# One decoder layer on one Trainium2 core: the eight buffers for the weights' high and low parts each made 32 bytes longer

## The chip, the core and the metric

The kernel is one program on one core of a Trainium2 chip. The metric is the device time of one execution in microseconds (us). Before the change three runs gave 1734.22, 1735.92 and 1740.03 us; their median is 1735.92 us. The profile shown below comes from one further execution of 1733.97 us.

## The reference, cut to what is computed

One layer of a decoder on 256 tokens with 2048 channels, in float32. A vector `c` gives shifts, scales and gates (`ada`); a first sub-layer mixes tokens by softmax attention and by a gated delta rule; a second one is a SwiGLU of width 5632.

```python
mod = silu(c) @ w_ada + b_ada
sh1, sc1, g1, sh2, sc2, g2 = split(mod, 6)
h = x * (1 + sc1) + sh1
proj = h @ w_in                               # 2048 x 13344
y_a = moba_attention(q, k, v, rel_bias)       # 8 heads of 128
y_b = gated_delta_rule(...) * silu(z)         # 16 heads of 128
merged = sigmoid(gate_a) * (y_a @ w_proj_moba) + sigmoid(gate_b) * (y_b @ w_proj_gdn)
x = layer_norm(ALPHA * x + g1 * (merged @ w_out))
h = x * (1 + sc2) + sh2
gate, up = split(h @ w_ffn_in, 2)
x = layer_norm(ALPHA * x + g2 * ((silu(gate) * up) @ w_ffn_out))
```

## The kernel before

**Steps.** The large products run as a list of 572 steps (`prog`, run by `run(3)`). A step takes one block of a weight matrix, at most 128 partitions x 1024 numbers: `load_w` starts its transfer into a buffer `raw` (five of them), ScalarE rounds it to the high part `hi` (line 211, type fp32r), VectorE computes the rest `lo = raw - hi` (line 212), and TensorE multiplies with both. There are four buffers for `hi` and four for `lo`, used in turn, so step n uses `hi` and `lo` number n modulo 4. `run(3)` keeps the preparation about three steps ahead of the products. ScalarE can write the next `hi` only after TensorE has read the buffer's last contents.

**Products.** A matmul on TensorE has a *stationary* operand (128 columns, brought in by a weight load, shown as PEld) and a *moving* one (256 or 512 columns). Three helpers use the buffers:

- `ws_mm` (lines 291, 292, 293): the weights `hi` and `lo` are stationary, activations move, 256 columns. Three matmuls for each piece: `hi` by the activation's high part, `hi` by its low part, `lo` by its high part. The first sub-layer runs mostly here, with activations in tiles that the profile calls `s` (the high and low parts of the layer's input), `ya` (attention), `ybA`, `ybBh` and `ybBl` (delta rule).
- `ws_wide` (lines 298, 302): again stationary weights, with the SwiGLU's input `h` moving; 512 columns with `hi` (high and low part of `h` side by side), 256 with `lo`.
- `xs_unit` (lines 339, 340, 341): the activations (`s`, `mh`, `ml`, `ach`, `acl`) are stationary, the weights `hi` and `lo` move, 512 or 256 columns.

**Other work.** The order of each engine's work follows the order of the code, and smaller work (the convolutions, the delta rule, the attention, the `ada` sums of line 231) is fed in between steps by `tick`. SyncE issues the weights' transfers; GpSimd issues small ones.

**Places.** The buffers lie in a pool `wp` in the order five `raw`, four `hi`, four `lo`, after the pool `perm` and before the pools of the stages. A buffer of 1024 numbers has 4096 bytes per partition, so all thirteen begin at the same place modulo 4096. In the built program the places of the tiles that are multiplied are these, in bytes modulo 256 (those of the first line are what the change touches):

| tile | begins at, modulo 256 | role in the products |
|---|---|---|
| `hi` 0 to 3, `lo` 0 to 3 | 64, all eight | stationary on lines 291 to 302, moving on 339 to 341 |
| `raw` 0 to 4 | 64 | read by lines 211 and 212 |
| `s`, `h`, `ya` | 128 | moving (291 to 302); `s` also stationary (339 to 341) |
| `ybA`, `ybBh` | 64 | moving |
| `ybBl` | 96 | moving |
| `mh`, `ml`, `ach`, `acl` | 64 | stationary |

The pieces of a tile that one matmul reads begin at multiples of 512 or 1024 bytes from the tile's start, so each has its tile's place. (Only the blocks of 768 and of 512 numbers are shorter; their pieces keep the place too.)

Of the kernel before, what the change touches and what calls it, by code (L numbers as in the profile page):

```python
# [11 lines left out]
F32R = mybir.dt.float32r  # L12
# [6 lines left out]
P = 128  # L19
# [73 lines left out]
def layer(ctx, tc, a, out):  # L93
# [5 lines left out]
    wp = ctx.enter_context(tc.tile_pool(name="wp", bufs=3))  # L99
# [105 lines left out]
        return v  # L205

    def split_w(raw, kn, cn, pin=False):
        hi = wp.tile([P, 1024], F32R, tag="hi", name="hi", bufs=4)
        lo = wp.tile([P, 1024], F32R, tag="lo", name="lo", bufs=4)
        hi, lo = [t[:, :kn * cn].rearrange("p (k n) -> p k n", n=cn) for t in (hi, lo)]  # L210
        s_.copy(hi, raw)  # L211
        low = v_.tensor_tensor(lo, raw, hi.bitcast(F32), op=OP.subtract)  # L212
        if pin:
            tc.keep_in_program_order(low)
        return hi, lo
# [49 lines left out]
    def step(w, k0, kn, c0, cn, post, begun=0, pin=False):  # L265
        prog.append((lambda: split_w(load_w(w, k0, kn, c0, cn), kn, cn, pin), post, begun))
# [1049 lines left out]
```

## Time and profile before

| | |
|---|---|
| median of three runs | 1735.92 us |
| profiled execution, its time | 1733.97 us |
| profiled execution, its span | 1732.2 us |
| VectorE `lo` of 128x1024 (line 212), one | 1221 ns, 512 times |
| ScalarE `hi` of 128x1024 (line 211), one | 1050 ns, 512 times |
| `raw` of 512 KB, issue to landing | 4.3 to 5.4 us |
| bytes moved by DMA | 418.47 MB |

A page of the profile lists busy time by engine, then the span in 40 slices of 43.3 us, then the chain of work that ended last, then groups of instructions by line. The view of stretches gives, for a window of time, the busy time of an engine and in brackets how many of its instructions touch the window. Records of matmuls overlap, because a matmul is pipelined: one of 256 columns has a record of about 0.28 us, though the next begins some 0.12 us after it. What a matmul costs in a dense stretch is therefore the distance between starts, and it is read as the window's length divided by the number of matmuls that begin in it.

### The profile page before, as it was taken

The numbers are of one execution on the slowest core, as the hardware profiler recorded it, in microseconds if no ns is written. First come the engines' busy times: TensorE is split into PE (matmuls) and PEld (weight loads), VectorE is DVE, ScalarE is ACT, GpSimd is POOL, SyncE is SP. The second block draws the span as 40 slices with busy tenths as digits, with TensorE's granted clock in tenths as the row PEclk, the third lists the DMA queues.
The fourth block names the chain that finished last, engine by engine and source line by source line (L and its number), as shares of the span: only waits on it lengthen the run. The fifth ranks groups of instructions, "written<-read, shape, count | busy, mean of one in ns | idle before, by whom it ended". The sixth has DMA issues, their size and how long they took to land.

```text
span 1732.2 us, 28121 instructions
## 1 busy us (share of the span) xinstructions
PE 1666.6 (96%) x11109; PEld 1516.0 (88%) x11109; DVE 1234.5 (71%) x1763; ACT 816.5 (47%) x1125; POOL 39.5 (2%) x61
## 2 busy tenths in 40 slices
PE   3899999999999999999999999999999999999997
PEld 3898999889999778999978998888888888888896
DVE  6899987899656687467986787666666655455454
ACT  3544445868535435464434454444444444433341
POOL 0000010110100101000000000000000000000000
PEclk9999999999999999999999999999999999999998
DMA  9999996565767668677998468777777766765652
GB/s 362 335 365 344 348 330 222 180 205 168 240 219 237 201 211 296 205 231 259 317 349 276 157 204 269 238 240 240 239 238 236 234 189 192 236 195 191 195 183 84
DMA packets 114532, 418.47 MB, mean 242 GB/s; under 512 B 13388, under 2 KB 14396, under 8 KB 108892
## 3 DMA queue, kind: packets, MB, share of 16 engines
q1 hardware_dynamic: 109888, 401.16, 68.7%
q0 software_dynamic: 4512, 15.51, 3.4%
q8 instruction: 87, 1.43, 0.3%
q14 instruction: 45, 0.37, 0.1%
HBM read 409.18 MB, written 7.44 MB: 241 GB/s over the span
## 4 chain that ended last, share of the span: by engine, by line
PE 78%; DMA 7%; DVE 7%; issue 6%; ACT 1%; POOL 0%; DVEq 0%; ACTq 0%; SPq 0%; POOLq 0%
PE mm L298 17%; PE mm L291 9%; PE mm L293 9%; PE mm L302 8%; PE mm L292 8%; PE mm L340 7%; PE mm L341 7%; PE mm L339 7%; DVE lo L212 3%; DMA raw_a<-in_w_ada 2%; DMA r<-in_w_ada 1%; PE ps L692 1%; DMA raw<-in_w_out 1%; DVE r L231 1%; ACT hi L211 1%
## 5 line engine op out<-in xcount | busy, mean ns | idle before, releaser
L211 ACT CAST hi<-raw 128x1024 fp32r<-128x1024 f32 (+2 forms) x572 | 581.6, 1020 | 777.5 <-PE mm L341 201.6
L212 DVE TENSOR_TENSOR lo<-raw,hi 128x1024 fp32r<-128x1024 f32 (+2 forms) x572 | 672.3, 1183 | 274.3 <-ACT hi L211 271.2
L291 PE MATMUL mm<-s,hi 128*128 128x256 f32 x1184 | 338.3, 286 | 6.3 <-ACT hi L211 6.1
L293 PE MATMUL mm<-s,lo 128*128 128x256 f32 x1184 | 332.9, 282 | 6.6 <-DVE lo L212 6.4
L292 PE MATMUL mm<-s,hi 128*128 128x256 f32 x1184 | 332.4, 281 | 0.0
L298 PE MATMUL mm<-h,hi 128*128 128x512 f32 x1280 | 319.0, 391 | 0.0
L298 PEld LDWEIGHTS mm<-h,hi 128*128 128x128 f32 x1280 | 228.8, 188 | 39.4
L291 PEld LDWEIGHTS mm<-s,hi 128*128 128x128 f32 x1184 | 224.7, 190 | 11.6 <-ACT hi L211 8.5
L293 PEld LDWEIGHTS mm<-s,lo 128*128 128x128 f32 x1184 | 223.7, 189 | 9.6 <-DVE lo L212 8.6
L292 PEld LDWEIGHTS mm<-s,hi 128*128 128x128 f32 x1184 | 224.7, 190 | 0.2
L302 PEld LDWEIGHTS mm<-h,lo 128*128 128x128 f32 x1280 | 171.1, 188 | 13.2
L302 PE MATMUL mm<-h,lo 128*128 128x256 f32 x1280 | 174.1, 278 | 0.0
L340 PE MATMUL mm<-lo,ach 128*128 128x512 f32 (+1 forms) x440 | 152.6, 347 | 0.2 <-DVE lo L212 0.2
L339 PE MATMUL mm<-hi,ach 128*128 128x512 f32 (+1 forms) x440 | 152.6, 347 | 0.0
L341 PE MATMUL mm<-hi,acl 128*128 128x512 f32 (+1 forms) x440 | 152.6, 347 | 0.0
L231 DVE CUSTOM_DVE_ANT_0 raw_a<-raw_a,cb,cols 128x1024 f32<-128x1024 f32 x56 | 71.8, 1282 | 73.9 <-DMA raw_a<-in_w_ada 73.9
L231 DVE CUSTOM_DVE_ANT_0 raw_a<-raw_a,cb,ada_half 128x1024 f32<-128x1024 f32 x56 | 71.8, 1282 | 66.0 <-DMA raw_a<-in_w_ada 65.8
L231 DVE CUSTOM_DVE_ANT_0 r<-r,cb,cols 128x2048 f32<-128x2048 f32 x40 | 93.8, 2346 | 13.4 <-DMA r<-in_w_ada 13.3
L340 PEld LDWEIGHTS mm<-lo,ach 128*128 128x128 f32 x440 | 83.3, 189 | 11.1 <-DVE lo L212 0.7
L339 PEld LDWEIGHTS mm<-hi,ach 128*128 128x128 f32 x440 | 83.3, 189 | 10.4
L341 PEld LDWEIGHTS mm<-hi,acl 128*128 128x128 f32 x440 | 83.3, 189 | 10.1
L340 PE MATMUL mm<-lo,s 128*128 128x512 f32 x192 | 77.4, 403 | 3.9 <-DVE lo L212 3.9
(299 smaller groups left out, 2310.6 us busy)
## 6 DMA issues: line engine op xcount, KB each, us to landing
raw<-in_w_ffn_in SPq DMA_DIRECT2D x176, 512.0 KB, 4.3
raw<-in_w_in SPq DMA_DIRECT2D x168, 512.0 KB, 4.6
raw_a<-in_w_ada SPq DMA_DIRECT2D x112, 512.0 KB, 4.5
raw<-in_w_ffn_out SPq DMA_DIRECT2D x88, 512.0 KB, 4.3
r<-in_w_ada SPq DMA_DIRECT2D x40, 1024.0 KB, 8.2
raw<-in_w_proj_gdn SPq DMA_DIRECT2D x32, 512.0 KB, 4.6
raw<-in_w_out SPq DMA_DIRECT2D x32, 512.0 KB, 5.4
raw<-in_w_in SPq DMA_DIRECT2D x40, 384.0 KB, 5.5
```

What stands on the lines that cost most here:

```text
L211: s_.copy(hi, raw)
L212: low = v_.tensor_tensor(lo, raw, hi.bitcast(F32), op=OP.subtract)
L231: v_.tensor_tensor_reduce(out=raw, in0=raw, in1=cb[:, n * part:n * part + n], scale=1.0, scalar=cols[:, col:col + 1] if first else h, op0= ...
L291: t_.matmul(o, hi[:, i, c], ah, start=(first and i == 0 and t == 0), stop=False)
L292: t_.matmul(o, hi[:, i, c], al, start=False, stop=False)
L293: t_.matmul(o, lo[:, i, c], ah, start=False, stop=(last and i == kn - 1 and t == 1))
L298: t_.matmul(box[t].rearrange("p (u i) -> p u i", u=2), hi[:, i, t * P:(t + 1) * P], both[k0 + i], start=(first and i == 0), stop=False)
L302: t_.matmul(box[t][:, :S], lo[:, i, t * P:(t + 1) * P], both[k0 + i][:, 0, :], start=False, stop=(last and i == kn - 1))
L339: t_.matmul(box[h], xh, hi[:, i, :], start=start, stop=False)
L340: t_.matmul(box[h], xh, lo[:, i, :], start=False, stop=False)
L341: t_.matmul(box[h], xl, hi[:, i, :], start=False, stop=stop)
L692: t_.matmul(ps[:, n, :], lhs(n), rhs(n), start=True, stop=True)
```

## The change

Each of the eight buffers for `hi` and `lo` gets 1032 numbers instead of 1024, that is 32 bytes more per partition. The steps use the first `kn * cn` numbers as before.

```diff
     def split_w(raw, kn, cn, pin=False):
-        hi = wp.tile([P, 1024], F32R, tag="hi", name="hi", bufs=4)
-        lo = wp.tile([P, 1024], F32R, tag="lo", name="lo", bufs=4)
+        hi = wp.tile([P, 1032], F32R, tag="hi", name="hi", bufs=4)
+        lo = wp.tile([P, 1032], F32R, tag="lo", name="lo", bufs=4)
         hi, lo = [t[:, :kn * cn].rearrange("p (k n) -> p k n", n=cn) for t in (hi, lo)]
         s_.copy(hi, raw)
         low = v_.tensor_tensor(lo, raw, hi.bitcast(F32), op=OP.subtract)
```

The places in the built program after it, modulo 256:

| tile | before | after |
|---|---|---|
| `hi` 0, 1, 2, 3 | 64, 64, 64, 64 | 64, 96, 128, 160 |
| `lo` 0, 1, 2, 3 | 64, 64, 64, 64 | 192, 224, 0, 32 |
| all other tiles | | the same place (those behind the pool lie 256 bytes further) |

On every engine and on both queues for transfers the instructions, their order, their sizes and the semaphores they wait for are the same as before; they differ in addresses alone.

## The prediction

> **What bounds the kernel now.** I read the page first, from the top, then the stretches of TensorE.
>
> ```profile
> PE 1666.6 (96%) x11109; PEld 1516.0 (88%) x11109; DVE 1234.5 (71%) x1763; ACT 816.5 (47%) x1125; POOL 39.5 (2%) x61
> ```
>
> Then its part on the chain of work that ended last:
>
> ```profile
> PE 78%; DMA 7%; DVE 7%; issue 6%; ACT 1%; POOL 0%; DVEq 0%; ACTq 0%; SPq 0%; POOLq 0%
> ```
>
> Then the view of stretches, TensorE alone (window, length, busy and count of matmuls, clock, DMA share, GB/s):
>
> ```profile
> 0.00:160.00 160.00, 124.35 (x958) 0.99 0.93 347
> 160.00:1010.00 850.00, 831.52 (x6084) 0.99 0.74 246
> 1010.00:1460.00 450.00, 449.61 (x2664) 1.00 0.73 233
> 1460.00:1710.00 250.00, 249.75 (x1346) 1.00 0.58 189
> ```
>
> TensorE is busy in 96% of the span, has 78% of the chain that ended last, and is granted a clock of 0.99 and 1.00 in the stretches below. These say where: in the first 160 us it is busy for 124, with the DMA engines at 0.93, so transfers set the pace there; in the next 1550 us it has 831.5 + 449.6 + 249.8 = 1531 of them. A change of a nanosecond in each matmul after 160 us is therefore a change in the time; one in VectorE or ScalarE is mostly covered.
>
> The change moves no instruction, so the only question is whether an instruction's duration depends on the *places* of its operands. The next rows answer that for today's places: dense stretches of one kind each.
>
> ```profile
> 208.00:280.00 72.00, 72.00 (x614) 1.00 0.85 298
> 187.00:200.00 13.00, 13.00 (x117) 1.00 0.94 348
> 282.00:292.00 10.00, 10.00 (x91) 1.00 0.59 177
> 618.00:660.00 42.00, 42.00 (x182) 1.00 0.75 240
> 836.00:841.00 5.00, 5.00 (x44) 1.00 0.96 312
> 914.00:952.00 38.00, 38.00 (x169) 1.00 0.82 273
> 953.00:975.00 22.00, 22.00 (x185) 1.00 0.59 192
> ...
> 1496.00:1652.00 156.00, 156.00 (x690) 1.00 0.62 200
> 1655.00:1665.00 10.00, 10.00 (x86) 1.00 0.51 172
> ```
>
> In order: `s` moving over stationary `hi`/`lo` (256 columns), the same again a little earlier and a little later, `hi`/`lo` moving over stationary `s` (512), `ybA` moving over `hi`/`lo` (256), `hi`/`lo` over `mh` (512, then 256), and over `ach` (512, then 256). Some 2.4 records of 0.28 us (1.7 of the 0.39 us ones) begin ahead of a window and count in it; I take them off. The distance between starts is then 72/611.6 = **117.7 ns**, 13/114.6 = **113.4**, 10/88.6 = **112.9**, 42/180.3 = **232.9**, 5/41.7 = **119.9**, 38/167.3 = **227.1**, 22/182.6 = **120.5**, 156/688.3 = **226.6**, 10/83.6 = **119.6**. The clock is 1.00 in all of them. So the same form of matmul runs at more than one pace. What goes with it is how the two operands lie to each other. Take the place modulo 128 and call 0 to 63 the lower half, 64 to 127 the upper one. Today `hi` and `lo` are all upper; `ybA`, `mh`, `ach` are upper as well, and with them the pace is constant, 120 and 226.7. `s`, `h` and `ya` are lower, and with them it is 117.7 or 113.4, and 232.9. The SwiGLU's steps show the last pairing, `h` (lower) moving over `hi` and `lo` (upper):
>
> ```profile
> 1201.53 1.07 PE L302 MATMUL mm<-h,lo 128*128 128x256 f32 x8
> 1202.44 1.99 PE L298 MATMUL mm<-h,hi 128*128 128x512 f32 x8
> 1204.27 1.11 PE L302 MATMUL mm<-h,lo 128*128 128x256 f32 x8
> ```
>
> Eight matmuls in a row of start and length; without the last record's own length the seven distances are (1.07 - 0.28)/7 = 113 ns, then (1.11 - 0.28)/7 = 119 (mean 116) in the next step, and (1.99 - 0.39)/7 = 229 for 512 columns. The pace alternates by step with equal operands modulo 256, so it also depends on how a stretch is entered. The halves are my reading of these rows, not a proof.
>
> **The change part by part.** VectorE and ScalarE first: they read `raw` and write `hi` and `lo` at new places.
>
> ```profile
> L211 ACT CAST hi<-raw 128x1024 fp32r<-128x1024 f32 (+2 forms) x572 | 581.6, 1020 | 777.5 <-PE mm L341 201.6 <-PE mm L298 199.2 <-PE mm L292 197.5
> ...
> L1027 DVE SCALAR_TENSOR_TENSOR r<-xs,rt 128x512 f32<-128x512 f32 (+1 forms) x10 | 5.8, 576 | 0.1
> ...
> L1027 DVE SCALAR_TENSOR_TENSOR r<-r,rt 128x512 f32<-128x512 f32 (+1 forms) x10 | 5.5, 578 | 0.1
> ```
>
> On line 1027, in the two stages that use it, one input of VectorE begins at 96 (`xs`) or at 128 (`r`): 576 and 578 ns. Places cost VectorE nothing within 2 ns; over 572 `lo` that is 1.1 us of either sign, and it lies under TensorE. ScalarE, of which no pair of rows differs in place alone, sits idle for 777.5 us ahead of line 211, mostly because TensorE still reads the buffer; over 572 `hi` it would have to lose more than 1.3 us in each to fill that. I take 0 for both. `raw` stays where it was, so its transfers cost 0 as well; in the first 160 us these hide whatever the 934 matmuls there gain or lose.
>
> For TensorE I carry the halves over. After the change `hi` 0, 1 and `lo` 0, 1 are upper (64, 96), `hi` 2, 3 and `lo` 2, 3 lower (0, 32), so half of the steps change their pairing. Counts are from these rows and their like (`ya`, `ybA`, `ybBh`, `ybBl` have 128 in each row, `h` on lines 291 to 293 112, `mm_kept` 96, `ach`/`acl` at 256 columns 176, `mh`/`ml` 96 and 64); the last row counts the matmuls with `s` of the first 160 us:
>
> ```profile
> L291 PE MATMUL mm<-s,hi 128*128 128x256 f32 x1184 | 338.3, 286 | 6.3 <-ACT hi L211 6.1
> L293 PE MATMUL mm<-s,lo 128*128 128x256 f32 x1184 | 332.9, 282 | 6.6 <-DVE lo L212 6.4
> L292 PE MATMUL mm<-s,hi 128*128 128x256 f32 x1184 | 332.4, 281 | 0.0
> L298 PE MATMUL mm<-h,hi 128*128 128x512 f32 x1280 | 319.0, 391 | 0.0
> L302 PE MATMUL mm<-h,lo 128*128 128x256 f32 x1280 | 174.1, 278 | 0.0
> ...
> L341 PE MATMUL mm<-hi,acl 128*128 128x512 f32 x264 | 102.7, 389 | 0.0
> L339 PE MATMUL mm<-hi,s 128*128 128x512 f32 x192 | 78.6, 411 | 0.3 <-ACT hi L211 0.3
> ...
> 0.00:160.00 160.00, 119.83 (x934) 0.99 0.93 347
> ```
>
> 1. `s`, `h`, `ya` over `hi`/`lo`, 256 columns: 3 x 1184 and 1008 like them are 4560, less the 934 of the first 160 us = 3626. Half go from unequal to equal halves: 1813 x (119.9 - 117.7 = 2.2 ns) = **+4.0 us**.
> 2. `h` over `lo`: 640 x (119.9 - 116 = 3.9 ns) = **+2.5 us**.
> 3. `h` over `hi`, 512: 640 x (226.7 - 229) = **-1.5 us**.
> 4. `ybA`, `ybB` (768): 384 from equal to unequal, x (-2.2) = **-0.8 us**.
> 5. `hi`/`lo` over `s` (576): 288 x (226.7 - 232.9) = **-1.8 us**.
> 6. `hi`/`lo` over `ach`, `acl`, `mh`, `ml`, 512 (1080): 540 from equal to lower moving over upper stationary, which is the pairing of `h` over `hi`, 229: 540 x 2.3 = **+1.2 us**.
> 7. The same with 256 columns (720): 360 x (-2.2) = **-0.8 us**.
>
> The sum is 4.0 + 2.5 - 1.5 - 0.8 - 1.8 + 1.2 - 0.8 = **+2.8 us**, so 1733.97 becomes 1736.8 in the terms of the profiled execution. That execution is 1.95 us below the median of the runs; against the median the forecast is 1735.92 + 2.8 = **1738.7 us**, no change that a measurement of this kernel can tell (about 0.3%, 5.2 us).
>
> Not in that sum is a start that is 32 bytes off a multiple of 64, which half of the buffers get. The nearest rows are a moving and a stationary operand at 96:
>
> ```profile
> 879.74 0.28 PE L292 MATMUL mm<-ybBl,hi 128*128 128x256 f32 x1
> ...
> 880.70 0.28 PE L291 MATMUL mm<-ybBh,hi 128*128 128x256 f32 x1
> ```
>
> ```profile
> L692 PEld LDWEIGHTS ps<-TT,ma 128*128 128x128 f32 (+1 forms) x128 | 11.8, 165 | 7.6 <-DVE kqn L583 4.2 <-ACT sgb L965 2.6 <-DMA TT<-ubd 0.4
> ...
> L692 PEld LDWEIGHTS ps<-UU,z 128*128 128x128 f32 (+1 forms) x128 | 11.5, 163 | 0.5
> ```
>
> With every third moving operand at 96 (`ybBl`), eight matmuls take 0.96 us, 120 ns each as with `ybA`; and a weight load of `z`, at 96, takes 163 ns against 165 for `ma` at 64. I take 0. But the first row has a pace with room in it (120, where 113.4 is possible) and the second is another type, so the price is open: up to one step between the paces seen, 119.9 - 113.4 = 6.5 ns, on one side, and on the other a gain of the same size where a stretch falls into the faster pace.
>
> A rule that speaks against any effect: the Trainium skill, page "SBUF — State Buffer", section "Who interferes with whom", gives TensorE two independent read ports, one for the moving operand and one for weight loads, and says that it never waits on anyone. By that rule the places are worth nothing and the time stays 1735.9; the rows above, 113.4 to 120 ns for one form at one clock, do not look like it.
>
> **The rivals.**
>
> *Places mean nothing.* The paces would come from the lengths and order of the stretches alone, and all terms are 0: 1735.9 us. For it: `s` over `hi` runs at both 117.7 and 113.4 with equal places. Against it: 120 and 226.7 appear only where the halves are equal.
>
> *Faster: the fast pace spreads.* Today a stretch at 117.7 keeps that pace for as long as it is dense (611 matmuls in the row at 208), because every step repeats the same places; with new places at each step the pace is chosen anew each time, as in the SwiGLU, where every other step has 113. If half of term 1's matmuls fall to 113.4: 1813 x -4.3 = -7.8, in place of +4.0, with the other terms at -1.2: 1735.9 - 9.0 = 1727 us. If all do: -15.6 - 1.2, 1719 us. It beats the 0.3% from about 900 of the 3626.
>
> *Slower: a start 32 bytes off costs.* Half of the 9330 matmuls that the seven terms count read a `hi` or `lo` at 32, 96, 160 or 224. At 3.25 ns, half of 6.5: 4665 x 3.25 = +15 us, with the sum of 2.8 it gives 1754 us; at the full 6.5 ns +30, 1769. With the +2.8 it passes 0.3% from (5.2 - 2.8)/4665 = 0.5 ns. Against it: the rows of `ybBl` and `z`. For it: they are the only ones, and neither is tight.
>
> *The change doesn't do what it says.* The places in the built program are the intended ones, and no other tile changes place; I give this nothing.
>
> **How the numbers follow.** Forecast 0.36; nothing at all 0.08; faster 0.26; slower 0.30. The first two are within 0.3%: 0.44 together. The predicted time is the forecast's, 1738.7. The range takes in the faster rival to 1720 and the slower one to 1758, a price of some 4 ns; beyond them I leave about 0.07 and 0.10. The forecast's own range is 1734 to 1741.
>
> **What would show it.** In the profile after, the count of matmuls in a dense stretch of `s` over `hi`/`lo` gives the pace by step: right if steps alternate in pairs between 118 and 120; the faster rival if many are at 113; the slower if steps with `hi` 1 and 3 differ from those with 0 and 2. `ach` at 512 should alternate between 227 and 229, `hi` over `s` between 233 and 227. Lines 211 and 212 should keep their mean (1020 ns for line 211) within 3 ns. Wrong would be a pace outside 113 to 120 and 226 to 236, or a longer line 212 that TensorE waits for.

## The result, and the profile after

| | before | after |
|---|---|---|
| median of the runs | 1735.21 us (1734.22 to 1740.03, 5 runs) | 1749.84 us (1748.46 to 1756.02, 5 runs) |
| profiled execution, its time | 1733.97 us | 1756.02 us |
| ratio, with its 95% interval | | 1.0073 (1.0051 to 1.0095) |

The changed kernel is slower by 14.6 us, 0.7%. The forecast was 1738.7 us, no change; the time lies in the range, on the side of the rival that had 0.30. The profiled execution is the slowest of the five, so its own 22 us over before hold some 7 that the median doesn't show.

The page after: first the span, the busy times and the chain of work that ended last.

```profile
span 1754.2 us, 28121 instructions
...
PE 1684.4 (96%) x11109; PEld 1524.8 (87%) x11109; DVE 1235.2 (70%) x1763; ACT 815.2 (46%) x1125; POOL 39.6 (2%) x61
...
PE 74%; DVE 9%; issue 8%; DMA 7%; ACT 1%; POOL 0%; SPq 0%; DVEq 0%; ACTq 0%; POOLq 0%
...
L211 ACT CAST hi<-raw 128x1024 fp32r<-128x1024 f32 (+2 forms) x572 | 580.9, 1019 | 800.4 <-PE mm L341 212.8
L212 DVE TENSOR_TENSOR lo<-raw,hi 128x1024 fp32r<-128x1024 f32 (+2 forms) x572 | 673.1, 1184 | 304.2 <-ACT hi L211 300.8
...
L298 PE MATMUL mm<-h,hi 128*128 128x512 f32 x1280 | 323.2, 394 | 0.0
...
L302 PE MATMUL mm<-h,lo 128*128 128x256 f32 x1280 | 176.8, 280 | 0.0
```

Same instructions, and TensorE alone has grown: 17.8 us more busy, while VectorE and ScalarE stay within 1.3. Lines 211 and 212 take 1019 and 1184 ns; they took 1020 and 1183. Lines 298 and 302, with no wait ahead of them before or after, take 394 and 280 ns in place of 391 and 278. A matmul's own duration overlaps the next, so its price is read from how many start in a stretch. Here are three stretches without idle time at a clock of 1.00, of before (window, length, busy and count, clock, DMA share, GB/s): `s` moving over `hi`/`lo` with 256 columns; the SwiGLU's, half 512 columns (`h` over `hi`) and half 256 (`h` over `lo`); `hi`/`lo` moving over `ach`/`acl` with 512.

```profile
213.00:279.00 66.00, 66.00 (x562) 1.00 0.84 295
1055.00:1470.00 415.00, 415.00 (x2412) 1.00 0.72 230
1500.00:1650.00 150.00, 150.00 (x664) 1.00 0.61 196
```

And of the changed kernel:

```profile
213.00:279.00 66.00, 66.00 (x557) 1.00 0.82 293
1055.00:1470.00 415.00, 415.00 (x2374) 1.00 0.72 229
1500.00:1650.00 150.00, 150.00 (x648) 1.00 0.59 197
```

With the records that began ahead of a window taken off as in the prediction (2.4, 2 and 1.7), one matmul takes 66/559.6 = 117.9 ns before and 66/554.6 = 119.0 after; 415/2410 = 172.2 and 415/2372 = 175.0; 150/662.3 = 226.5 and 150/646.3 = 232.1. The SwiGLU alone loses 2.8 ns x 2560 = 7 us, about half of the 14.6. Below, these three windows serve as the measure of every kernel, and "the three paces" are worked out from them in this way.

### The profile page after: what moved, and what is told of

It is laid out like the page before. It is cut to its first block, busy times and chain, and to the rows that moved or that the text cites. A ratio compares the mean times of both kernels' runs of the same rounds, so it can differ in the third digit from the quotient of the medians.

```text
span 1754.2 us, 28121 instructions
## 1 busy us (share of the span) xinstructions
PE 1684.4 (96%) x11109; PEld 1524.8 (87%) x11109; DVE 1235.2 (70%) x1763; ACT 815.2 (46%) x1125; POOL 39.6 (2%) x61
## 4 chain that ended last, share of the span: by engine, by line
PE 74%; DVE 9%; issue 8%; DMA 7%; ACT 1%; POOL 0%; SPq 0%; DVEq 0%; ACTq 0%; POOLq 0%
PE mm L298 17%; PE mm L302 9%; PE mm L291 8%; PE mm L293 8%; PE mm L292 7%; PE mm L340 7%; PE mm L341 7%; PE mm L339 7%; DVE lo L212 3%; DMA raw_a<-in_w_ada 2%; PE ps L692 1%; DVE r L231 1%; DMA raw<-in_w_out 1%; DMA raw<-in_w_proj_gdn 1%; DMA r<-in_w_ada 1%
## 5 line engine op out<-in xcount | busy, mean ns | idle before, releaser
L211 ACT CAST hi<-raw 128x1024 fp32r<-128x1024 f32 (+2 forms) x572 | 580.9, 1019 | 800.4 <-PE mm L341 212.8
L212 DVE TENSOR_TENSOR lo<-raw,hi 128x1024 fp32r<-128x1024 f32 (+2 forms) x572 | 673.1, 1184 | 304.2 <-ACT hi L211 300.8
L298 PE MATMUL mm<-h,hi 128*128 128x512 f32 x1280 | 323.2, 394 | 0.0
L293 PEld LDWEIGHTS mm<-s,lo 128*128 128x128 f32 x1184 | 224.2, 190 | 11.1 <-DVE lo L212 10.1
L302 PEld LDWEIGHTS mm<-h,lo 128*128 128x128 f32 x1280 | 173.6, 188 | 13.7
L231 DVE CUSTOM_DVE_ANT_0 r<-r,cb,cols 128x2048 f32<-128x2048 f32 x40 | 93.7, 2347 | 12.3 <-DMA r<-in_w_ada 12.3
L340 PEld LDWEIGHTS mm<-lo,ach 128*128 128x128 f32 x440 | 82.8, 188 | 11.7
L341 PEld LDWEIGHTS mm<-hi,acl 128*128 128x128 f32 x440 | 82.7, 188 | 11.7
```

What stands on the lines that cost most here:

```text
L231: v_.tensor_tensor_reduce(out=raw, in0=raw, in1=cb[:, n * part:n * part + n], scale=1.0, scalar=cols[:, col:col + 1] if first else h, op0= ...
L293: t_.matmul(o, lo[:, i, c], ah, start=False, stop=(last and i == kn - 1 and t == 1))
L298: t_.matmul(box[t].rearrange("p (u i) -> p u i", u=2), hi[:, i, t * P:(t + 1) * P], both[k0 + i], start=(first and i == 0), stop=False)
L302: t_.matmul(box[t][:, :S], lo[:, i, t * P:(t + 1) * P], both[k0 + i][:, 0, :], start=False, stop=(last and i == kn - 1))
L340: t_.matmul(box[h], xh, lo[:, i, :], start=False, stop=False)
L341: t_.matmul(box[h], xl, hi[:, i, :], start=False, stop=stop)
```

## The experiments

Three theories were on record. 'Halves' is the forecast's: what counts is in which half of 128 bytes the two operands begin. 'Offset' is the slower rival's: a start that is no multiple of 64 costs. 'Variety' (later 'changing places'): the places as such cost nothing, but going to another one does. The edits below are against the kernel before; `gap(tag, n)` allocates once a tile of n elements of 4 bytes that nothing reads or writes, so what lies behind it moves.

### Only the later tiles move (gap256)

```
     lo = wp.tile([P, 1024], F32R, tag="lo", name="lo", bufs=4)
+    gap("gap2", 64)
```

> An unused tile of 256 bytes lies behind the eight buffers, which themselves keep their places (all at 64 modulo 256); every other tile lies exactly where the change puts it. It asks whether the 256 bytes by which the later pools moved have a part in the loss. Theory 'offset' (a start that is not a multiple of 64 bytes costs), theory 'variety' (it costs when the place changes from one operand to the next) and theory 'halves' (equal or unequal halves of 128 bytes) all expect 0 against before (within 0.2%). If it shows the change's +0.7%, all three fall.

Measured: 1736.85 us against 1736.88, ratio 0.9999 (0.9984 to 1.0015). The SwiGLU's window:

```profile
1055.00:1470.00 415.00, 415.00 (x2412) 1.00 0.72 228
```

The same count as before. The 256 bytes by which the change pushes other tiles have no part in the loss.

### All eight at 96, all eight at 128 (all96, all128)

```
+    gap("gap0", 8)
     hi = wp.tile([P, 1024], F32R, tag="hi", name="hi", bufs=4)
     lo = wp.tile([P, 1024], F32R, tag="lo", name="lo", bufs=4)
+    gap("gap2", 56)
```

That is all96; all128 has 16 and 48.

> All eight buffers at one place, 96 modulo 256; all other tiles as in the changed kernel. Offset: the change has half of its buffers off a multiple of 64 and lost 14.6 us, so with all of them off it loses about 29 us (+1.7%). Variety: all operands of a kind have one place again, 0 (within 0.3%), with a constant pace in each stretch. Halves: 96 lies in the upper half as 64 does, 0.

> All eight buffers at one place, 128 modulo 256; all other tiles as in the changed kernel. Offset: 0. Variety: 0. Halves: all eight change from the upper to the lower half, twice the seven terms of the prediction, 2 x 2.8 = +5.6 us (+0.3%), with a pace of 120 ns for 256 columns of s over hi, 226.7 ns for hi over s at 512 columns and 229 ns for hi over ach.

Measured: at 96 1744.31 us, ratio 1.0039 (1.0024 to 1.0055), +7.4 us; at 128 1746.96, ratio 1.0063 (1.0043 to 1.0083), +10.1 us. The windows at 96:

```profile
213.00:279.00 66.00, 66.00 (x569) 1.00 0.82 292
1055.00:1470.00 415.00, 415.00 (x2373) 1.00 0.71 226
1500.00:1650.00 150.00, 150.00 (x645) 1.00 0.59 196
```

And at 128:

```profile
213.00:279.00 66.00, 66.00 (x552) 1.00 0.83 292
1055.00:1470.00 415.00, 415.00 (x2381) 1.00 0.71 228
1500.00:1650.00 150.00, 150.00 (x657) 1.00 0.60 194
```

The three paces are 116.5, 175.0, 233.2 at 96, and 120.1, 174.4, 228.9 at 128. No theory stands whole. Nothing changes between steps, yet both are slower, so 'variety' is not all. 'Halves' is right that 96 and 128 differ, and for `s` (equal halves at 128: 120) and `ach` (unequal: 229), but not in its 0 for 96. 'Offset' is right for `ach` at 512 columns, where 96 costs the full step of 6.7 ns over 226.5, and wrong for `s` at 256, where 96 is faster than 64 (116.5 against 117.9); hence +7 and not +29.

### `hi` in steps of 64, `lo` at 64 (hi64steps)

```
-    hi = wp.tile([P, 1024], F32R, tag="hi", name="hi", bufs=4)
+    hi = wp.tile([P, 1040], F32R, tag="hi", name="hi", bufs=4)
```

> hi alone in four places that are all multiples of 64 bytes (64, 128, 192, 0 modulo 256); lo at 64 in all four buffers; all other tiles as in the changed kernel. Offset: 0, no start is off a multiple of 64. Variety: two of three matmuls read hi, so the larger part of the change's loss, +7 to +14 us (+0.4 to 0.8%). Halves: the terms of hi alone, about 0.

Measured: 1741.1 us, ratio 1.0024 (1.0007 to 1.0041), +4.2 us. Two of its windows, `s` and `ach`:

```profile
213.00:279.00 66.00, 66.00 (x572) 1.00 0.84 296
...
1500.00:1650.00 150.00, 150.00 (x649) 1.00 0.60 195
```

`s` at 66/569.6 = 115.9 ns is faster than before, `ach` at 231.7 slower, though no start is off a multiple of 64. It lies between the theories; it doesn't tell whether the places or their change do it.

### All at 160; and two places in turn (all160, alt192, alt128, alt96)

all160 is all96 with 24 and 40 elements. The other three give even steps one place and odd steps another (`count` begins as `[0]`):

```
+    par = count[0] % 2
+    count[0] += 1
+    if par:
+        gap("gap1", 32)
-    hi = wp.tile([P, 1024], F32R, tag="hi", name="hi", bufs=4)
-    lo = wp.tile([P, 1024], F32R, tag="lo", name="lo", bufs=4)
+    hi = wp.tile([P, 1024], F32R, tag=f"hi{par}", name="hi", bufs=2)
+    lo = wp.tile([P, 1024], F32R, tag=f"lo{par}", name="lo", bufs=2)
+    if par:
+        gap("gap2", 32)
```

That is alt192 (64 and 192); alt128 has 16 and 48, alt96 8 and 56.

> All eight buffers begin at 160 (32 modulo 128): 32 bytes off a multiple of 64, as 96 is, but in the lower half of 128, as 128 is. Theory 'own place, offset': what counts is whether the start is a multiple of 64; 160 then behaves as 96 did: 116.7 ns a matmul at 256 columns and 233.3 at 512 throughout, +7 us over before. Theory 'own place, half': the half of 128 counts, and 160 behaves as 128 did: 119 to 120 ns for s, h and ya, 118 for ach, 228 to 230 at 512, +10 us. Theory 'changing places' says nothing of this kernel, in which no step differs from the next.

> Both parts of even steps at 64, of odd steps at 192: the place changes by 128 bytes with each step. Theory 'own place modulo 128': the two are the same place, 0 us, paces as before (117.4 for s, 226.8 for ach at 512, 233.3 over s). Theory 'own place modulo 256': 192 is a place not seen yet, and something other than 0. Theory 'changing places' in its wide form (any change of buffer place between two steps breaks up the pace that a stretch keeps): +8 us, what the changed kernel lost (+14) beyond the mean of its places (about +6). In its narrow form (only a change modulo 128 counts): 0.

> Both parts of even steps at 64, of odd steps at 128. Theory 'own place': half of the steps cost what all of them cost with all eight at 128 (+10 us), so +5 us, and the paces are the mean of the two: 118.6 for s at 256 columns, 227.9 for ach at 512. Theory 'changing places': that and some 8 us more, +13 us, with ach at 512 at 230 or above, though neither place alone gives more than 229.

> Both parts of even steps at 64, of odd steps at 96. Theory 'own place': half of what all eight at 96 cost (+7 us), so +3.7 us; s at 117.1, ach at 512 at 230, the mean of 226.8 and 233.3. Theory 'changing places': some 8 us more, +12 us; s at 118 or above, though neither place alone gives more than 117.4.

Measured, with the ratio: all160 1750.17 us, 1.0087 (1.0062 to 1.0111), +13.6; alt192 1739.4, 1.0022 (1.0004 to 1.0039), +2.8; alt128 1740.81, 1.0021 (1.0008 to 1.0035), +4.2; alt96 1744.72, 1.0054 (1.0036 to 1.0071), +8.1. The windows at 160:

```profile
213.00:279.00 66.00, 66.00 (x560) 1.00 0.83 294
1055.00:1470.00 415.00, 415.00 (x2361) 1.00 0.72 227
1500.00:1650.00 150.00, 150.00 (x644) 1.00 0.61 194
```

The paces are 118.4, 175.9, 233.5: at 512 columns those of 96, as 'offset' had it, at 256 between those of 96 and 128; in time it is the slowest place measured. The SwiGLU and `ach` with 64 and 192 in turn:

```profile
1055.00:1470.00 415.00, 415.00 (x2383) 1.00 0.71 227
1500.00:1650.00 150.00, 150.00 (x653) 1.00 0.60 194
```

with 64 and 128 in turn:

```profile
1055.00:1470.00 415.00, 415.00 (x2398) 1.00 0.72 228
1500.00:1650.00 150.00, 150.00 (x652) 1.00 0.61 194
```

and with 64 and 96:

```profile
1055.00:1470.00 415.00, 415.00 (x2389) 1.00 0.72 227
1500.00:1650.00 150.00, 150.00 (x650) 1.00 0.61 197
```

For 64 and 128 the mean of the two places alone would be 173.3 and 227.7; measured are 415/2396 = 173.2 and 150/650.3 = 230.7. For 64 and 96: 173.6 and 229.8; measured 173.9 and 231.4. In time the means are +5.0 and +3.7, measured +4.2 and +8.1. So 'own place' holds for the SwiGLU; at 512 columns over `ach` the alternation adds 1.6 to 3 ns. In time 64 and 128 come out as 'own place' says. 64 and 96 lie between the theories: the interval, 6.2 to 12.3 us, leaves out the 3.7 of 'own place' and takes in the 12 of 'changing places'. Nor does `s` keep to the mean. Its window with 64 and 192 in turn, then with 64 and 128:

```profile
213.00:279.00 66.00, 66.00 (x581) 1.00 0.85 297
```

```profile
213.00:279.00 66.00, 66.00 (x568) 1.00 0.85 296
```

That is 114.1 ns, as with all eight at 192 (below), and 116.7, faster than 64 alone and 128 alone (117.9 and 120.1).

alt192 is not 0 in its paces (174.3 and 230.3): either 192 is not the place that 64 is, or the change by 128 bytes does it. The next kernel separates these.

### All at 192; a place for each stage (all192, bystage)

all192 is all96 with 32 and 32 elements. bystage gives each step an offset into longer buffers that all begin at 64 (in elements: 32 is place 192, 16 is 128, 8 is 96):

```
-    def split_w(raw, kn, cn, pin=False):
-        hi = wp.tile([P, 1024], F32R, tag="hi", name="hi", bufs=4)
-        lo = wp.tile([P, 1024], F32R, tag="lo", name="lo", bufs=4)
-        hi, lo = [t[:, :kn * cn].rearrange("p (k n) -> p k n", n=cn) for t in (hi, lo)]
+    def split_w(raw, kn, cn, pin=False, at=(32, 32)):
+        hi = wp.tile([P, 1088], F32R, tag="hi", name="hi", bufs=4)
+        lo = wp.tile([P, 1088], F32R, tag="lo", name="lo", bufs=4)
+        hi, lo = [t[:, o:o + kn * cn].rearrange("p (k n) -> p k n", n=cn) for t, o in zip((hi, lo), at)]
...
+            n = 8 if cn == 256 else 16 if ops is h_ops else 0
-            step(w, k0, kn, c0, cn, post)
+            step(w, k0, kn, c0, cn, post, at=(n, n))
...
-            step(w_fi, k, 4, c0, 256, post)
+            step(w_fi, k, 4, c0, 256, post, at=(0, 32))
...
-    nc = bacc.Bacc("TRN2", target_bir_lowering=False, num_devices=1, dynamic_dma_scratch_size=4096)
+    nc = bacc.Bacc("TRN2", target_bir_lowering=False, num_devices=1, dynamic_dma_scratch_size=2304)
```

> All eight buffers begin at 192, which is 64 modulo 128, so that no step differs from the next. Theory 'own place modulo 128': the same place as before, 0 us, paces as before (s at 256 columns 117.4 ns, ach at 512 226.8, h at 512 228.9). Theory 'own place modulo 256': the paces that the steps at 192 had where places alternated, now throughout: s 114.6, ach at 512 232.6, h at 512 233.0, s at 512 229.5; 3637 x -2.8 for s, 1637 x -0.6 for h, 366 x -2.7 for ya and 762 x -1.7 for yb are -13.5 us, 791 x 5.8, 270 x 4.3, 1280 x 4.1 and 526 x -3.8 are +9.0, together about -5 us. Theory 'changing places': what 64 and 192 in turn cost came from the change, so 0 us here.

> A place for each stage, the same for all its steps: 192 where hi and lo are the stationary part at 256 columns (s, ya, yb, h over lo), 96 where they move at 256 columns, 128 where they move over s at 512, 64 for the other 512-column matmuls, as before. The buffers are 256 bytes longer for it, and the descriptor ring of the DMA queue of POOL smaller. Theory 'own place': the paces add up by place: 3637 x -2.8 ns for s, 366 x -2.7 for ya, 762 x -1.7 for yb, 1637 x -0.6 for h are -13.5 us, less 934 x 2.8 = 2.6 that the transfers of the first 160 us hide; 718 x -3.3 at 96 -2.4, 526 x -5.6 at 128 -2.9: -16 us, about 1720. Theory 'own place modulo 128': 192 is 64, so only the last two terms, -5 us. Theory 'changing places': the place changes only where a stage ends, so as 'own place' says.

Measured: all192 1739.87 us, ratio 1.0021 (0.9996 to 1.0045), +4.3; bystage 1733.59, ratio 0.9976 (0.9954 to 0.9998), -2.0. The windows at 192:

```profile
213.00:279.00 66.00, 66.00 (x581) 1.00 0.85 297
1055.00:1470.00 415.00, 415.00 (x2395) 1.00 0.72 229
1500.00:1650.00 150.00, 150.00 (x647) 1.00 0.59 194
```

The paces are 114.1, 173.4, 232.5, without any change between steps: 192 is not 64, though the two are equal modulo 128. That ends 'halves'. The time does not follow these paces: 'own place modulo 256' expected about -5 us, and the distances, summed over all groups of matmuls, are about 6 us shorter than before, but the time is +4.3 us (interval -0.7 to +7.8).

Nor does a place alone fix the pace of `s`. A later stretch of all192, again `s` over `hi`/`lo` and nothing else:

```profile
704.00:727.00 23.00, 23.00 (x198) 1.00 0.63 211
```

This is 23/195.6 = 117.6 ns, the pace that `s` mostly has at 64; and the prediction has a row at 64 with 113.4. In the records of both kernels a long dense stretch of `s` has the one pace or the other from its start to its end. At 192 the faster comes more often: the mean over all records of `s` is 115.0 ns there and 117.4 at 64. At 96, 128 and 160 (116.9, 119.9, 118.3) no such pair of paces shows.

The windows of bystage:

```profile
213.00:279.00 66.00, 66.00 (x581) 1.00 0.86 297
1055.00:1470.00 415.00, 415.00 (x2420) 1.00 0.73 232
1500.00:1650.00 150.00, 150.00 (x663) 1.00 0.61 197
```

`s` at 192 has 114.1 here as well, and `ach` at 64 has 226.8, as before, though these buffers lie at other addresses and 256 bytes further apart: the place modulo 256 can be chosen for each stage, and the mean pace comes with it (over all records `s` has 115.3 here). Summed over all groups of matmuls, the distances between starts are 18 us shorter than before (counted as in the table of terms further down). But of the 16 us expected the runs show 2. The stage from 442 to 788 us, where the GDN heads are worked off between the projections, in bystage:

```profile
442.00:788.00 346.00, 326.29 (x2408) 0.98 0.70 227
```

and before:

```profile
442.00:788.00 346.00, 334.32 (x2440) 0.99 0.72 230
```

TensorE is busy for 8 us less there and still gets through 32 matmuls fewer. The waits of TensorE (waiter, what it waited for: us in total, times, longest) name the largest new one, in bystage:

```profile
PE ps L693 <- DMA TT<-ubd: 12.5, 2, 9.6
```

The same line before:

```profile
PE ps L692 <- DMA TT<-ubd: 0.2, 1, 0.2
```

That is 12.3 us more. The granted clock falls in the stretch of the longest of these waits, of bystage:

```profile
670.00:683.00 13.00, 3.88 (x19) 0.61 0.96 336
```

The mean granted clock of its timed runs was lower too, 0.987 against 0.991 for the kernel before beside it; its fastest run, 1720.34 us, is the one with 0.993.

Faster matmuls reach the transfer earlier, but it is not shown that this is the whole reason for the wait: this kernel also has the smaller descriptor ring of POOL's queue, on which the transfer is issued. Two issues of GpSimd (start, length, the issue, idle time before it), in bystage:

```profile
667.91 0.90 POOL L684 DMA_DIRECT2D UU<-ubd  x1 [6.96 <-issue]
668.80 0.90 POOL L684 DMA_DIRECT2D TT<-ubd  x1
```

And before:

```profile
665.20 0.91 POOL L683 DMA_DIRECT2D UU<-ubd  x1
670.06 0.89 POOL L683 DMA_DIRECT2D TT<-ubd  x1 [3.95 <-DMA ubd<-mt]
```

In bystage both transfers come after 6.96 us of idle time for which the profile shows no cause, one right behind the other. All three kernels with the smaller ring (the next two have it too) show such idle time there, 6.0 to 7.0 us, and the longest waits for `TT`, 9.8 to 12.5 us; no kernel with the old ring shows it, and their waits are at most 7.0 us (6.9 in all192). So the ring is a rival for a part of the lost gain. A run with the longer buffers and the old ring was not made.

### The changed kernel's places, changing each step or every eighth (each1, each8)

```
...
+    at = 8 * (count[0] % 4)
+    count[0] += 1
-    hi = wp.tile([P, 1024], F32R, tag="hi", name="hi", bufs=4)
-    lo = wp.tile([P, 1024], F32R, tag="lo", name="lo", bufs=4)
-    hi, lo = [t[:, :kn * cn].rearrange("p (k n) -> p k n", n=cn) for t in (hi, lo)]
+    hi = wp.tile([P, 1088], F32R, tag="hi", name="hi", bufs=4)
+    lo = wp.tile([P, 1088], F32R, tag="lo", name="lo", bufs=4)
+    hi, lo = [t[:, o:o + kn * cn].rearrange("p (k n) -> p k n", n=cn) for t, o in ((hi, at), (lo, at + 32))]
...
-    nc = bacc.Bacc("TRN2", target_bir_lowering=False, num_devices=1, dynamic_dma_scratch_size=4096)
+    nc = bacc.Bacc("TRN2", target_bir_lowering=False, num_devices=1, dynamic_dma_scratch_size=2304)
```

That is each1; each8 has `8 * (count[0] // 8 % 4)`.

> The places of the changed kernel in another way: the eight buffers begin at 64, and step n reads and writes hi at 64 + 32 x (n mod 4) and lo 128 bytes further on, which are the changed kernel's places step by step. (Buffers 256 bytes longer, the descriptor ring of POOL's DMA queue smaller, as in the kernel with a place for each stage.) All theories: as the changed kernel, +13 us, s at 118.4 ns, ach at 512 at 232.2, h at 512 at 232.2, s at 512 at 232.2. A time nearer to before would say that something else than the places made the changed kernel slower, or that the ring matters.

> The same four pairs of places, equally often, but each kept for eight steps before the next. Theory 'own place': nothing changes, as the kernel that goes to the next place with each step: +13 us, ach at 512 at 232, s at 118.4. Theory 'changing places': seven of eight changes are gone, and with them some 4 of the about 5 us that the changed kernel lost beyond the mean of the places measured alone (64, 96, 128, 160: 0, +7, +10, +14; mean +8): +9 us, with ach at 512 nearer to the mean of those four, 230.6 ns, than to 232.2.

Measured: each1 1756.71 us, ratio 1.0112 (1.0087 to 1.0138), +20.8; each8 1754.7, ratio 1.0097 (1.0064 to 1.0131), +18.8. The SwiGLU and `ach` in each1:

```profile
1055.00:1470.00 415.00, 415.00 (x2364) 1.00 0.73 230
1500.00:1650.00 150.00, 150.00 (x650) 1.00 0.62 201
```

and in each8:

```profile
1055.00:1470.00 415.00, 415.00 (x2377) 1.00 0.72 229
1500.00:1650.00 150.00, 150.00 (x647) 1.00 0.62 196
```

The places alone, given to the steps in another way, reproduce the paces: 175.7 and 231.4 (changed kernel: 175.0 and 232.1). In time both came out 4 to 6 us above the changed kernel; TensorE's wait for `TT` is long in them as well (11.7 us and 9.8, against 7.0 in the changed kernel), and that part, with the ring, stays open.

What going to another place with each step costs, the times can't tell: the 2 us between the two lie within the intervals. The traces tell more. Summed as in the table of terms below, the distances are longer than before by about 14 us in each1, 11 in each8, and 9 in the mean of the kernels with all eight at 64, 96, 128 and 160. So some 3 of the 5 us beyond that mean go with the change at each step, as 'changing places' had it. The SwiGLU shows it (175.7 in each1, 174.7 in each8, 174.4 in the mean); `ach` does not, at 232.5 in each8. There the single steps of each8 show where the rest lies: with `hi` at 96 and at 160 they take 233.3 and 233.2 ns, as with all eight there, but with `hi` at 64 and `lo` at 192 231.0 instead of 226.8, and with `hi` at 128 and `lo` at 0 230.4 instead of 228.9. As each pair stays for eight steps, this goes with the other place of `lo`.

## Why the prediction was wrong in size, step by step

| all eight at, modulo 256 | `s`, 256 | SwiGLU, 512 and 256 | `ach`, 512 | time against before |
|---|---|---|---|---|
| 64 (before) | 117.9 ns | 172.2 ns | 226.5 ns | 0 |
| 96 | 116.5 | 175.0 | 233.2 | +7.4 us |
| 128 | 120.1 | 174.4 | 228.9 | +10.1 |
| 160 | 118.4 | 175.9 | 233.5 | +13.6 |
| 192 | 114.1 | 173.4 | 232.5 | +4.3 |
| mean of 64 to 160 | 118.2 | 174.4 | 230.5 | +7.8 |
| the changed kernel | 119.0 | 175.0 | 232.1 | +14.6 |

The paces are those of the three windows; the time of the kernel at 192 is not clear of 0 (interval -0.7 to +7.8 us).

The prediction's first step holds for this change: the loss lies in the distance between TensorE's matmuls (13.3 of the 14.6 us, next table), that distance depends on the places, and VectorE and ScalarE don't mind them. It does not hold for every kernel: where the matmuls got faster (all192, bystage), the time gained little or nothing. The rival in which places mean nothing is refuted by all96, all128 and all160, and with it what the prediction drew from the rule quoted there (the Trainium skill, page "SBUF — State Buffer", section "Who interferes with whom": two independent ports, TensorE never waits on anyone): by that reading 226.5 and 233.2 ns would be one number. The rule itself speaks of engines that wait for one another and names no places; whether a wait at a port stands behind these paces, no run here shows.

The terms are set against the profile of the changed kernel in the next table. "Measured" is the mean distance between the starts of successive matmuls over all records of the trace (distances over 150 ns at 256 columns and 260 at 512, which hold waits, left out), after less before, times the count before. Term 1 as measured takes in the matmuls of the first 160 us, which the forecast left out; without them it is about +3.3.

| term | forecast | measured |
|---|---|---|
| 1. `s`, `ya`, 256 | +4.0 us | 3637 x 1.0 + 366 x 0.7 = +3.9 us |
| 2. `h` over `lo`, with `h` of lines 291 to 293 | +2.5 | 1637 x 2.0 = +3.3 |
| 3. `h` over `hi`, 512 | -1.5 | 1280 x 3.3 = +4.2 |
| 4. `ybA`, `ybB` | -0.8 | 762 x -1.8 = -1.4 |
| 5. `hi`/`lo` over `s`, 512 | -1.8 | 530 x -1.1 = -0.6 |
| 6. `hi`/`lo` over `ach`, `mh`, 512 | +1.2 | 791 x 5.4 + 270 x 3.9 = +5.3 |
| 7. the same, 256 | -0.8 | 718 x -1.9 = -1.4 |
| sum | +2.8 | +13.3 |

**Terms 3 and 6** are where it failed: 9.8 of the 10.5 us that the sum is short, and both are 512-column terms. Two steps behind them were wrong.

The first is "I take 0" for a start 32 bytes off a multiple of 64. For `ach` at 512 columns its price is the upper bound that the prediction had kept for the range, 6.5 ns, or a little more: at 96 and at 160 it runs at 233.2 and 233.5. At 256 there is no common price: over all records `s` has 116.9 and 118.3 at 96 and 160 against 117.4, `h` over `lo` 116.7 and 118.9 against 115.8. Nor is it the offset as such, since 192, a multiple of 64, runs `ach` at 232.5. The rows from which 0 was taken were both of 256 columns or fewer, and the price was carried over to 512 without a row there. This is near the slower rival's mechanism, but at 512 columns alone; a loss that doubles with the buffers that are off would have made 29 us for all96, and that kernel lost 7. The sign that the prediction had named for it came at 512 columns: in the changed kernel `h` over `hi` takes 234.2 and 233.1 ns a matmul with `hi` 1 and 3, 230.9 and 230.7 with 0 and 2.

The second is the halves, which came from rows at one place of `hi` and `lo`. They put `h` over `hi` at 128 to 226.7; with all eight there the records give 230.1, against 228.9 before, and the SwiGLU is slower than at 64, not faster. And 192, in the same half as 64, runs `ach` at 232.5. The two paces that the prediction gave to equal halves, 120 and 226.7, go with equal places modulo 256 instead. At 256 columns equal places have 119.9 or 120.0 ns over all records (`ybA` and `ach` at 64, `s` and `ya` at 128); at 512 columns with the activations stationary they have the fastest pace (`ach` at 64 226.8, `s` at 128 227.7). With `hi` and `lo` at 96, the same half but not the same place, `ach` has 116.7 and 233.3. This orders the rows but is no rule: `h` over `hi` is slower with equal places (230.1) than at 64 (228.9), and `ach` at 256 columns has 120.0 at 160 too. That term 1 came out so near is in part luck.

**The faster rival** had its mechanism in the wrong place: `s` does spread to the faster pace, 114.1 ns at 192, and 115.9 in hi64steps. But of the changed kernel's four places for `hi` none is 192, the mean is 119.0, and no 48 matmuls of `s` in a row average below 115.8. Even where the paces came (bystage), the time gained 2 of 18 us.

**What is shown and what stays open.** That the places make the changed kernel slower is shown by gap256 (0 without them) and each1 (its paces with them alone). The time fell in the prediction's range because that range took in the slower rival; its forecast of no change failed. The mean of the four places of `hi`, each measured alone, gives 7.8 of the 14.6 us, and 2.2 of the 2.8 ns in the SwiGLU. Of the rest, a part goes with the change from step to step (each1 against each8, by the traces) and a part with `lo`, which has other places than `hi` (the steps of each8); `lo` at 224, 0 and 32 was in no kernel alone. Why a place has its pace, and what decides which of its two paces a stretch of `s` takes at 64 and at 192, is not known from these runs.

## What to carry to other kernels

In a kernel like this one, where TensorE runs densely for most of the span, the start of its operands modulo 256 is a parameter like any other: here it moves the pace by up to 3% at 512 columns and 5% at 256, in opposite directions for different products, so measure it for each product instead of carrying a rule over from one width to another. Padding that staggers buffers is not free of effect: no kernel here with places that differ from buffer to buffer was faster than before. And before counting a gain in the pace, look for the waits that lie just behind it, and change nothing else along with it: 18 us of faster matmuls in the trace became 2 us of time, in a kernel that also had a smaller descriptor ring.

## What the runs showed of the hardware

- The distance between dense matmuls at a granted clock of 1.00 depends on where the operand begins modulo 256 bytes: 114.1 to 120.1 ns for `s` over `hi`/`lo` at 256 columns, 226.5 to 233.5 ns for `hi`/`lo` over `ach` at 512.
- One place can have two paces: `s` at 64 ran at 113.4 (187 to 200 us) and 117.9 ns (213 to 279 us) in the kernel before, at 192 at 114.1 (213 to 279 us) and 117.6 ns (704 to 727 us) in all192.
- The best place for one product is among the worst for another: 192 has the fastest `s` (114.1) and nearly the slowest `ach` (232.5).
- Starts at 96 and 160 cost `ach` at 512 columns (233.2 and 233.5 against 226.5 at 64), but so does 192 (232.5); `s` at 256 has 116.5 and 118.4 against 117.9.
- In bystage a long gap in TensorE's work and a lower granted clock came together: 0.61 in the 13 us around a wait of 9.6 us. Its mean clock was 0.987 over its runs, against 0.991 for the kernel before beside it.
